# Modulation steps issued one by one behind weight tiles, and z gates multiplied in full float32

## The chip, the cores and the metric

The kernel runs on one core of a Trainium2 chip, as one program. The metric is the time of one execution in microseconds (us); a median of three runs is given with the lowest and the highest. All of the engines' times come from a profile of one execution.

## The reference, cut to what matters

Two blocks work on 256 tokens of width 1024. The first block has two layers. Each layer is a norm, one wide projection, three mixers beside each other, and an output projection. The mixers are an attention with compressed, selected and windowed keys (nsa), a linear recurrence (lru) and a convolution (conv). Each mixer's output is gated by its own `z` columns of the same wide projection:

```
h = rms_norm(x, norm_g[l]);  cols = h @ w_in[l]          # z_nsa, z_lru, z_conv among the columns
mixed = concat([y_nsa * silu(z_nsa), y_lru * silu(z_lru), y_conv * silu(z_conv)])   # 512 columns each
x = x + mixed @ w_out[l]
```

The second block starts from a modulation. It depends only on the conditioning vectors, not on x, and so can be computed at any time before the second block needs it:

```
mod_lat = silu(c) @ w_ada + b_ada         # 6 parts of 1024: sh1, sc1, gt1, sh2, sc2, gt2
mod_ctx = silu(c_ctx) @ w_ada + b_ada     # the same weights
h_lat = rmsnorm(x, g_norm1) * (1 + sc1) + sh1;   h_ctx = rmsnorm(ctx, g_norm1) * (1 + csc1) + csh1
x = x + gt1 * mixers(h_lat, h_ctx);   h2 = rmsnorm(x, g_norm2) * (1 + sc2) + sh2
x = x + gt2 * peer(h2)                    # 16 of 16384 expert rows per head and token, gathered
```

## The kernel before, in words

Activations lie transposed: 8 blocks of 128 channels (k) by 256 tokens. A weight tile is 128 x 1024 float32, 512 KB: for 128 output columns, all 8 k. SP issues every load of it (`wload`, L310 to L316), into five raw buffers (`w`); modulation tiles have two buffers of their own (`wm`).

Products of layers are made in three passes of a faster precision, fp32r. The norm's output is split into a high part `hh` and a low part `hl` (`norm_apply`, L449), and each weight tile likewise (`wsplit`, L318): ScalarE casts it to `wh` (L323), VectorE subtracts that from the raw tile into `wl` (L268). `mm3` (L350) then makes hh·wh, hh·wl and hl·wh for each k, 24 products per tile. A split leaves the raw buffer free as soon as both engines have read it; there are three buffers for each half.

A layer has 40 such tiles: glu, kv, q and u (20, for the mixers), z (12, in six `zpair`s, L755) and the output projection `woa` (8), whose remaining part `wob` (for the convolution) comes as four tiles of another shape. Between them stand the attention's small float32 products, the convolution's taps on VectorE (L262), its norm, and the scan of the recurrence.

The modulation's five parts that TensorE computes (`part`, L958) have 8 steps each: one 512 KB tile of `w_ada` per step and four products of 32 columns, one in each column group of the array, with `silc` (the activated conditioning vectors) as stationary operand; then a copy, two transposes and an addition that put the part into `modt`. (The sixth part is summed on VectorE from tiles in the raw buffers.)

The order on every engine is set by a scheduler that runs through the program's instructions by priority, a time that the code writes down (`at`, L246), and moves them by its own timeline of engines and loads. Before the change the parts had times of their own, `P["mt"]`, taken by a hook of the layers (L1665): the first three parts at 62, 80 and 170, the last two at 243 and 270. A loaded tile's priority lies 25 us (`ll`) ahead of its use, a split's 6 us (`sl`). `slot` hands out named places in memory in turn: `g6` holds the norm's whole output until it is split, and later the split input of `wob` (`mch`, `mcl`).

Of the kernel before, what the change touches and what calls it, by code (L numbers as in the profile page):

```python
# [9 lines left out]
F32R = mybir.dt.float32r  # L10
# [9 lines left out]
T = 256  # L20
# [209 lines left out]

P = dict(np=5, glu=14, kv=35, kk=40, q=41, cmp=46, cmpd=5, w1n=62, cv0=32, cvd=35, att=57, attd=5, mix=137, woa=131, ln=145, pw2=160, wob=138, mod=5, ll=25000, sl=6000, nm=3, mt=(62, 80, 170, 243, 270), sp=29, L0=10, L1=196, S=369, B=500, cx=125, h1=2, h2=6, X=16, lri=37, lnk=7, tp=2, tq=0, ta=0, ml=40, mld=2.6, rt=36, g0=-32, ga=104, gb=161, gc=157)

# [6 lines left out]
def program(tc, A, dbg=lambda *a: None, stop=99):  # L241
# [11 lines left out]
        return p.tile(list(shape), dt, name=f"{tag}_{cnt[0]}", tag=tag, **kw)  # L253

    def mm(out, lhsT, rhs, start, stop):
        pe.matmul(out, lhsT, rhs, start=start, stop=stop)  # L256

    def tr(out, in_, ident):
        pe.transpose(out, in_, ident)  # L259
# [90 lines left out]
    def mm3(out, pairs, first=True, last=True, late=False):  # L350

        n = len(pairs)
        for i, (ah, al, bh, bl) in enumerate(pairs):
            mm(out, ah, bh, first and i == 0, False)
            if late:
                mm(out, al, bh, False, False)
            else:
                mm(out, ah, bl, False, False)
                mm(out, al, bh, False, last and i == n - 1)
        if late:  # L360
            for i, (ah, al, bh, bl) in enumerate(pairs):
                mm(out, ah, bl, False, last and i == n - 1)

    def rsqrt(p, v, shape, tag, bufs=2):

# [80 lines left out]
    hh = mk(cp, [128, 8, T], F32R, tag="hh")  # L446
    hl = mk(cp, [128, 8, T], F32R, tag="hl")

    def norm_apply(p, src, gain, shift=None, hi=None, lo=None, bc=None):  # L449
        if bc is None:  # L450
            bc = norm_rstd(p, [src[:, k] for k in range(8)], D)
        g6 = None if hi is not None else slot("g6", 2048).rearrange("p (k t) -> p k t", k=8)
        if hi is None:
            hi, lo = hh, hl
        p0 = tc.cur_priority
        for k in range(0, 8, 2):
            tc.cur_priority = p0
            t = mk(p, [128, 2, T], tag="tmp2", bufs=2) if g6 is None else g6[:, k:k + 2]
            for q in range(2):
                scaled[:] = [dve.scalar_tensor_tensor(t[:, q], src[:, k + q], gain[:, k + q:k + q + 1], bc, op0=mul, op1=mul)]  # L460
            if shift is None:
# [12 lines left out]
        return last  # L474
# [88 lines left out]
    def layer(l, L, hook=lambda n: None):  # L563
# [8 lines left out]
        def proj2(i, t=None):  # L572

            acc = psum("acc", [128, 2, T])
            for q in range(2):
                if t is not None:
                    at(L + t + 2.6 * q)
                wh, wl = wsplit(A["w1"][l, i + q], [128, 8, 128])
                mm3(acc[:, q], [(wh[:, k], wl[:, k], hh[:, k], hl[:, k]) for k in range(8)], late=i == 0)
            if t is not None:  # L580
                at(L + t + 5.2)
            return acc
# [170 lines left out]
        gzc = slot("gz4", 1024).rearrange("p (i t) -> p i t", i=4)  # L753

        def zpair(i):  # L755
            acc = proj2(20 + i)
            th = mk(b1, [128, 2, T], tag="tmp2", bufs=2)
            act.activation(th, acc, AF.Tanh, scale=0.5)
            stt(gz[:, i:i + 2] if i < 8 else gzc[:, i - 8:i - 6], th, 1.0, acc, add, mul)
# [81 lines left out]
            onat.append(oT)  # L841


        g6 = slot("g6", 2048, F32R).rearrange("p (w i t) -> p w i t", w=2, i=4)
        mch, mcl = g6[:, 0], g6[:, 1]

        def pick(i):
            return (hh, hl, i) if i < 8 else (mch, mcl, i - 8)

        def msplit(i, src):  # L850
            h, lo, j = pick(i)
# [68 lines left out]
        for n in range(0, 8, 2):  # L920
            acc = psum("acc", [128, 2, T])
            for q in range(2):
                at(L + P["woa"] + 2.6 * (n + q))
                wh, wl = wsplit(A["woa"][l, n + q], [128, 8, 128])
                mm3(acc[:, q], [(wh[:, k], wl[:, k], hh[:, k], hl[:, k]) for k in (4, 5, 6, 7, 0, 1, 2, 3)])
            stt(XT[:, n:n + 2], acc, 0.5, XT[:, n:n + 2], mul, add)
            for c in order.pop(0):
                steps[c]()

        for n2 in range(4):  # L930
            at(L + P["wob"] + 2.6 * n2)
            wh, wl = wsplit(A["wob"][l, n2], [128, 4, 256])
            acc = psum("acc", [128, 2, T])
            for q in range(2):
                s = slice(q * 128, q * 128 + 128)
                mm3(acc[:, q], [(wh[:, k, s], wl[:, k, s], mch[:, k], mcl[:, k]) for k in range(4)])
            stt(XT[:, n2 * 2:n2 * 2 + 2], acc, 0.5, XT[:, n2 * 2:n2 * 2 + 2], mul, add)
# [6 lines left out]
    def modulation():  # L944

        sc = slot("silc", 256).rearrange("p (k w) -> p k w", k=8)

        def prep():
            nc.sync.dma_start(pb2, A["pb2"])
            cT = P2("c").rearrange("p (k w) -> p k w", w=2)  # L950
            pool.memset(sc, 0.0)
            s2 = sc[:, :, 0:2]
            act.activation(s2, cT, AF.Tanh, scale=0.5)
            stt(s2, s2, 1.0, cT, add, mul)
            ts(s2, s2, 0.5, None, mul)
            act.activation(sc0, sc[:, :, 0], AF.Copy)

        def part(m):  # L958
            acc = psum("c", [128, 256])
            for k in range(8):  # L960
                w = wload(A["wada"][m, k], [128, 4, 256], "wm", NWM, b1)
                for j in range(4):
                    pe.matmul(acc[32 * j:32 * j + 32], sc[:, k], w[:, j], start=k == 0, stop=k == 7,  # L963
                              tile_position=(0, 32 * j))
            rows = slot("ang", 256)
            act.activation(rows, acc, AF.Copy)
            tp = psum("c", [128, 2, 128])
# [12 lines left out]

        return [prep] + [lambda m=m: part(m) for m in (1, 0, 2, 4, 3)[:int(P["np"])]]

    def modsum(acc, m, k):

# [5 lines left out]
            stt(acc, w, s, acc, mul, add)  # L990

    def modparts():
        for m in (4, 3)[int(P["np"]) - 3:]:
            acc = mk(b1, [128, 1024], tag="wm", bufs=NWM)
            for k in range(8):
                modsum(acc, m, k)
# [661 lines left out]
            pass  # L1658
        pp.release()

    steps = modulation()
    at(P["mod"])
    steps.pop(0)()

    def hook(n, l):  # L1665
        if n == 0:
            if l == 1:
                next(two)
            return
        for i in range(min(int(P["nm"]), len(steps)) if l == 0 else len(steps)):  # L1670
            at(P["mt"][int(P["np"]) - len(steps)])
            steps.pop(0)()

    layer(0, P["L0"], lambda n: hook(n, 0))
    two = second(P["L1"] + P["cx"], P["S"])
# [18 lines left out]
```

## Time and profile before

| | us |
|---|---|
| median of 3 runs | 1381.29 (1377.42 to 1384.13) |
| the profiled execution | 1384.02, its span 1382.2 |
| TensorE (PE) busy | 1193.9, 86% of the span, mean granted clock 0.946 |
| VectorE (DVE) busy | 991.6, 72% |
| ScalarE (ACT) busy | 530.5, 38% |
| moved by DMA | 387.5 MB, 280 GB/s in the mean; 268.45 MB of it gathered expert rows |

The execution falls into parts: layer 0 up to about 248 us, layer 1 up to about 469, the second block's mixers up to about 640, then the experts. A busy share over the whole span mixes these; the table of stretches below separates them. A product's duration in the timeline overlaps the next one's, so the cost of one is read from start to start. A float32 product of TensorE appears as two records, an fp32r product as one.

### The profile page before, as it was taken

The page shows a single profiled execution, that of the slowest core. Times are in us where ns is not written, and L with a number is a line of the kernel's source. Part 1 is how long each engine was busy: PE and PEld are TensorE (multiplying, and loading weights), DVE is VectorE, ACT ScalarE, POOL GpSimd, SP SyncE. Part 2 cuts the span into 40 slices and gives each one's busy share as a digit, 9 for nine tenths or more (in the row PEclk, how much of TensorE's full clock was granted, in tenths as well). Part 3 has the DMA queues.
Part 4 walks back from the last instruction along what each step waited for, and adds up shares of the span by engine and source line. Part 5 has one row for each costly group of instructions (what it writes and reads, how often), then busy time and mean ns, then how long its engine had stood idle before and what let it go on. Part 6 is the DMA issues. An engine that isn't in the chain of part 4 may idle for free.

```text
span 1382.2 us, 17743 instructions
## 1 busy us (share of the span) xinstructions
PE 1193.9 (86%) x5972; PEld 775.5 (56%) x5972; DVE 991.6 (72%) x2440; ACT 530.5 (38%) x1136; POOL 296.2 (21%) x279
## 2 busy tenths in 40 slices
PE   6999889899979999999898877778887878778776
PEld 5987659698947986658794323343333333323332
DVE  6898865599988676566678776777766767676554
ACT  5635643344755555554543212222212222212211
POOL 0000000000000000000024444434453444444441
PEclk9999999899999999999999999999899999999999
DMA  8587454547413442401479999999999999999996
GB/s 321 196 282 274 158 183 168 197 158 264 137 41 100 153 130 83 146 16 46 138 313 387 422 422 421 421 409 384 421 414 422 421 419 397 424 421 398 421 422 263
DMA packets 71340, 387.50 MB, mean 280 GB/s; under 512 B 8402, under 2 KB 9426, under 8 KB 38227
## 3 DMA queue, kind: packets, MB, share of 16 engines
q0 software_dynamic: 36864, 268.45, 47.1%
q1 hardware_dynamic: 34386, 117.93, 24.7%
q8 instruction: 48, 0.79, 0.2%
q14 instruction: 42, 0.34, 0.1%
HBM read 385.30 MB, written 1.05 MB: 280 GB/s over the span
## 4 chain that ended last, share of the span: by engine, by line
PE 48%; DMA 30%; DVE 8%; issue 7%; POOL 4%; ACT 2%; POOLq 0%; DVEq 0%; SPq 0%; ACTq 0%
DMA G<-uv,eix 27%; PE acc L256 22%; PE acx L256 11%; PE s L256 5%; POOL G L1583 4%; DVE G L1586 4%; DMA wm<-wada 2%; PE c L963 2%; PE t L256 2%; PE o L256 2%; PE s L412 1%; PE t L259 1%; PE c L256 1%; PE o L811 1%; PE o L645 1%
## 5 line engine op out<-in xcount | busy, mean ns | idle before, releaser
L1586 DVE SCALAR_TENSOR_TENSOR G<-G,hn 128x1024 f32<-128x1024 f32 x256 | 313.4, 1224 | 177.3 <-DMA G<-uv,eix 170.2
L1583 POOL DMA_INDIRECT G<-uv,eix x256 | 288.7, 1128 | 438.8 <-PE acx L256 140.6
L268 DVE TENSOR_TENSOR wl<-w,wh 128x1024 fp32r<-128x1024 f32 (+2 forms) x142 | 171.4, 1209 | 69.8 <-ACT wh L323 68.3
L323 ACT ACTIVATE wh<-w 128x1024 fp32r<-128x1024 f32 (+2 forms) x142 | 148.5, 1048 | 188.1 <-PE acc L256 115.7
L256 PE MATMUL t<-G,dg 128*128 128x512 f32 x256 | 146.5, 656 | 70.1 <-ACT dg L1599 70.1
L256 PE MATMUL c<-G,dg 128*128 128x512 f32 x256 | 148.1, 663 | 62.4 <-ACT dg L1599 62.4
L256 PE MATMUL acc<-hh,wh 128*128 128x256 f32 x608 | 178.5, 297 | 7.8 <-ACT hh L468 3.6
L256 PE MATMUL acc<-hh,wl 128*128 128x256 f32 x608 | 176.8, 293 | 2.7 <-DVE wl L268 2.0
L256 PE MATMUL acc<-hl,wh 128*128 128x256 f32 x608 | 166.5, 287 | 1.2 <-DVE hl L268 1.1
L1599 ACT ACTIVATE dg<-cst,w 128x128 f32<-128x128 f32 x256 | 89.4, 394 | 149.1 <-PE o L256 64.4
L256 PE MATMUL acx<-G,dg 128*128 128x512 f32 x256 | 143.1, 643 | 0.0
L256 PE MATMUL o<-G,dg 128*128 128x512 f32 x256 | 141.2, 635 | 0.0
L1590 ACT ACTIVATE s<-s 128x4 f32<-128x4 f32 (+1 forms) x66 | 13.5, 205 | 325.2 <-DVE G L1586 325.2
L256 PEld LDWEIGHTS t<-G,dg 128*128 128x128 f32 x256 | 50.2, 206 | 149.9 <-ACT dg L1599 96.0
L256 PEld LDWEIGHTS acc<-hh,wh 128*128 128x128 f32 x608 | 119.3, 197 | 16.2 <-issue 4.7
L256 PEld LDWEIGHTS c<-G,dg 128*128 128x128 f32 x256 | 50.5, 209 | 135.1 <-ACT dg L1599 83.3
L256 PEld LDWEIGHTS acc<-hh,wl 128*128 128x128 f32 x608 | 119.7, 197 | 7.1 <-DVE wl L268 2.9
L256 PEld LDWEIGHTS acc<-hl,wh 128*128 128x128 f32 x608 | 113.8, 193 | 5.8 <-issue 3.2
L262 DVE SCALAR_TENSOR_TENSOR g<-lu,pb,g 128x256 f32<-128x256 f32 x264 | 115.0, 476 | 0.2
L256 PEld LDWEIGHTS o<-G,dg 128*128 128x128 f32 x256 | 53.2, 208 | 69.9 <-issue 69.9
L256 PEld LDWEIGHTS acx<-G,dg 128*128 128x128 f32 x256 | 52.7, 206 | 69.0 <-issue 69.0
L1054 POOL MEMSET lu<- 128x16 f32 x1 | 0.4, 447 | 401.9 <-DVE g L262 401.9
(512 smaller groups left out, 1947.6 us busy)
## 6 DMA issues: line engine op xcount, KB each, us to landing
w<-w SPq DMA_DIRECT2D x64, 512.0 KB, 4.6
wm<-wada SPq DMA_DIRECT2D x40, 512.0 KB, 4.5
wa<-cw SPq DMA_DIRECT2D x16, 512.0 KB, 5.1
w<-woa SPq DMA_DIRECT2D x16, 512.0 KB, 3.5
w<-wpq SPq DMA_DIRECT2D x16, 512.0 KB, 3.5
w<-w2t SPq DMA_DIRECT2D x12, 512.0 KB, 3.5
w<-wob SPq DMA_DIRECT2D x8, 512.0 KB, 4.6
w<-w2v SPq DMA_DIRECT2D x8, 512.0 KB, 3.8
```

Source lines behind the costliest of these rows:

```text
L256: pe.matmul(out, lhsT, rhs, start=start, stop=stop)
L259: pe.transpose(out, in_, ident)
L262: (e or dve).scalar_tensor_tensor(out, a, s, b, op0=op0, op1=op1)
L268: return (e or dve).tensor_tensor(out, a, b, op=op)
L323: act.activation(hi, w, AF.Copy)
L412: pe.matmul(acc[j:j + 32], ones[:, 0:32], sq[:, q] if square else srcs[i + q], start=i + q < 4, stop=i + q >= n - 4, tile_position=(0, j))
L645: pe.matmul(hps[32 * j:32 * j + 32], blk[:, q4 * 4 + j], w[:, j], start=q4 == 0, stop=q4 == 3, tile_position=(0, 32 * j))
L811: pe.matmul(ops[gs, jj:jj + step], vsw[kb][:, bi - 1, gs], p4[:, :, g, kb], start=bi == 1 and kb == 0 and jj == 0, stop=False, tile_positi ...
L963: pe.matmul(acc[32 * j:32 * j + 32], sc[:, k], w[:, j], start=k == 0, stop=k == 7, tile_position=(0, 32 * j))
L1583: pool.indirect_dma_start(out=G, out_offset=None, in_=A["uv"], in_offset=bass.IndirectOffsetOnAxis(ap=eix[b][:, h, k:k + 1], axis=0))
L1586: dot = dve.scalar_tensor_tensor(G[:, 0:D], G[:, 0:D], 1.0, hn[b], op0=mul, op1=mul, accum_out=s[:, j:j + 1])
L1599: act.activation(dg, ident, AF.Copy, scale=w[:, j:j + 1])
```

## The change

The z gates' tiles are no longer split. `zpair` loads the raw tile and multiplies it by the norm's unsplit output (`whole[0]`, the `g6` place), in float32: 8 products per tile, no cast and no subtraction. `g6` is therefore needed longer, and `mch` and `mcl` are allotted at their first use, not earlier.

The modulation loses its times. It becomes a list of 45 steps (`modq`: 40 of products, 5 ends of parts); after two of every three tiles of `w1`, z and `woa`, `fill` takes one step off the list and issues it right behind that tile's last product. Each step issues the load of the tile two steps ahead; the first two loads stand at the start of layer 0. The computation is otherwise the same. The core of the diff (`P` loses np, nm and mt; `mm` and `mm3` return their last instruction):

```diff
+    modq, tiles_done = [], [0]
+    def fill(end):
+        tiles_done[0] += 1
+        if modq and tiles_done[0] % 3:
+            p = tc.cur_priority
+            with tc.issue_after(end.ins):
+                modq.pop(0)()
+            tc.cur_priority = p
...
+        whole[:] = [g6]                                   # in norm_apply
...
-                mm3(acc[:, q], [(wh[:, k], wl[:, k], hh[:, k], hl[:, k]) for k in range(8)], late=i == 0)
+                fill(mm3(acc[:, q], [(wh[:, k], wl[:, k], hh[:, k], hl[:, k]) for k in range(8)], late=i == 0))
...
         def zpair(i):
-            acc = proj2(20 + i)
+            acc = psum("acc", [128, 2, T])
+            for q in range(2):
+                w = wload(A["w1"][l, 20 + i + q], [128, 8, 128])
+                for k in range(8):
+                    end = mm(acc[:, q], w[:, k], whole[0][:, k], k == 0, k == 7)
+                fill(end)
...
+        order = [(m, k) for m in (1, 0, 2, 4, 3) for k in range(8)]
+        def load():
+            if order:
+                m, k = order.pop(0)
+                loaded.append(wload(A["wada"][m, k], [128, 4, 256], "wm", NWM, b1))
+        def products(m, k):
+            if k == 0:
+                accs[m] = psum("c", [128, 256])
+            w = loaded.pop(0)
+            for j in range(4):
+                pe.matmul(accs[m][32 * j:32 * j + 32], sc[:, k], w[:, j], start=k == 0, stop=k == 7,
+                          tile_position=(0, 32 * j))
+            load()
         def part(m):
-            acc = psum("c", [128, 256])
-            for k in range(8):
-                w = wload(A["wada"][m, k], [128, 4, 256], "wm", NWM, b1)
-                for j in range(4):
-                    pe.matmul(acc[32 * j:32 * j + 32], sc[:, k], w[:, j], start=k == 0, stop=k == 7,
-                              tile_position=(0, 32 * j))
+            acc = accs[m]
...
-    steps.pop(0)()
+    prep()
+    at(P["L0"] + P["glu"])
+    load()
+    load()
+    modq.extend(steps)
```

What this does to the order is seen at three places. In the rows, `c<-wm,silc` is a product of a modulation step, `acc` and `acx` are accumulations of weight tiles, `s`, `t` and `o` pieces of the attention and the norms. The first place is TensorE's queue in layer 0's tail before the change, behind the last z tile: the start of the third modulation part.

```order
L256 MATMUL s_1738<-g_10_86 128x512
L256 LDWEIGHTS identb_74
L256 MATMUL s_1738<-cmaskb_76,identb_74 128x2x128
L963 MATMUL c_1216<-wm_1217,silc_103 32x256 x2
L811 MATMUL o_1272<-pTs_1554,vsw_1075 64x256 x2
L963 MATMUL c_1216<-wm_1217,silc_103 32x256 x2
L963 MATMUL c_1216<-wm_1223,silc_103 32x256 x4
L256 MATMUL s_1763<-g_10_86 128x512
L256 LDWEIGHTS identb_74
L256 MATMUL s_1763<-cmaskb_76,identb_74 128x2x128
L963 MATMUL c_1216<-wm_1229,silc_103 32x256 x4
L963 MATMUL c_1216<-wm_1235,silc_103 32x256 x4
```

There the steps of a part stand close together, whole, between pieces of the attention. After the change the second step of the same part stands further ahead, in the tenth z tile of layer 0 (`g_37_163` is the unsplit norm output, `w_1641` the raw tile).

```order
L256 MATMUL acc_1624<-g_37_163,w_1641 128x256
L999 MATMUL c_1614<-wm_1522,silc_103 32x256
L256 MATMUL acc_1624<-g_37_163,w_1641 128x256
L999 MATMUL c_1614<-wm_1522,silc_103 32x256
L256 MATMUL acc_1624<-g_37_163,w_1641 128x256
L999 MATMUL c_1614<-wm_1522,silc_103 32x256
L256 MATMUL acc_1624<-g_37_163,w_1641 128x256
L999 MATMUL c_1614<-wm_1522,silc_103 32x256
L256 MATMUL acc_1624<-g_37_163,w_1641 128x256
L832 MATMUL o_1435<-pTs_1487,vsw_1169 64x128 x4
L259 MATMUL t_1543<-cst_62,pr_1499 128x128 x4
```

The step is cut into its four products, each between two of the tile's products. The second place is the boundary of the layers in TensorE's queue, before the change: the last products of layer 0, the norm's sums and its scaling (`t<-dg`), and the first tile of layer 1.

```order
L963 MATMUL c_3634<-wm_3647,silc_103 32x256 x4
L963 MATMUL c_3634<-wm_3653,silc_103 32x256 x4
L412 MATMUL s_2674<-tmp_435_2685,cst_62 32x256 x2
L412 MATMUL s_2674<-tmp_436_2690,cst_62 32x256 x2
L256 MATMUL s_2697<-cst_62,tmp_2695 128x1 x2
L963 MATMUL c_3634<-wm_3659,silc_103 32x256 x4
L963 MATMUL c_3634<-wm_3665,silc_103 32x256 x4
L256 MATMUL t_2716<-dg_2717,cst_62 128x128
L256 MATMUL t_2716<-dg_2720,cst_62 128x128
L963 MATMUL c_3634<-wm_3671,silc_103 32x256 x4
L256 MATMUL acc_2740<-hh_81,wh_2743 128x256
```

Four steps of a part stand within the norm's chain there, and another ahead of the next layer's first product. The same place after the change:

```order
L256 MATMUL acc_2412<-g_355_1994,wl_2410 128x256
L424 MATMUL s_2438<-tmp_413_2449,cst_62 32x256 x2
L424 MATMUL s_2438<-tmp_414_2454,cst_62 32x256 x2
L256 MATMUL s_2461<-cst_62,tmp_2459 128x1 x2
L256 MATMUL t_2480<-dg_2481,cst_62 128x128
L256 MATMUL t_2480<-dg_2484,cst_62 128x128
L256 MATMUL acc_2504<-hh_81,wh_2507 128x256
L256 MATMUL acc_2504<-hh_81,wl_2509 128x256
```

The norm's chain stands alone; the steps have moved behind tiles of layer 1.

## Rows read from the trace of the kernel before

**Rows 1.** The page, chain that ended last: shares by engine, by line.

```profile
PE 48%; DMA 30%; DVE 8%; issue 7%; POOL 4%; ACT 2%; POOLq 0%; DVEq 0%; SPq 0%; ACTq 0%
DMA G<-uv,eix 27%; PE acc L256 22%; PE acx L256 11%; PE s L256 5%; POOL G L1583 4%; DVE G L1586 4%; DMA wm<-wada 2%; PE c L963 2%; PE t L256 2%; PE o L256 2%; PE s L412 1%; PE t L259 1%; PE c L256 1%; PE o L811 1%; PE o L645 1%
```

**Rows 2.** Stretches of core 0: busy time of each engine in each.

```profile
core 0: us, PE busy (x) PEld busy (x) DVE busy (x) ACT busy (x) POOL busy (x), PEclk, DMA share, GB/s
19.20:158.80 139.60, 139.58 (x1117) 120.14 (x1118) 123.55 (x271) 76.68 (x144) 0.00 (x0) 1.00 0.68 237
158.80:204.40 45.60, 38.11 (x309) 19.87 (x307) 34.34 (x113) 22.38 (x59) 0.00 (x0) 0.90 0.59 206
...
248.20:262.40 14.20, 9.61 (x70) 4.23 (x69) 9.05 (x27) 4.52 (x8) 0.00 (x0) 0.67 0.68 234
262.40:384.30 121.90, 121.90 (x978) 112.65 (x974) 110.07 (x226) 66.34 (x128) 0.00 (x0) 1.00 0.52 175
384.30:407.50 23.20, 15.29 (x76) 8.86 (x76) 21.36 (x63) 12.61 (x28) 0.45 (x1) 0.85 0.12 39
407.50:433.80 26.30, 23.12 (x172) 14.60 (x171) 18.43 (x67) 16.52 (x47) 0.00 (x0) 1.00 0.15 50
```

**Rows 3.** The chain, 158 to 206, then 206 to 265: start, us, what.

```profile
by line: DMA wm<-wada 37.6%; PE c L963 17.7%; PE s L256 14.6%; PE t L259 6.2%; PE o L811 6.1%; PE o L256 4.0%; PE acc L256 4.0%; PE s L412 2.3%; ACT pr L794 2.1%; PE acx L256 2.0%; PE c L259 1.8%; ACT ang L966 0.8%; issue 0.8%
...
by line: PE acc L256 52.9%; PE acx L256 22.2%; DMA wm<-wada 15.2%; PE c L963 8.0%; PE s L412 1.8%; issue 0.2%
...
217.39 11.51 PE acc L256 x96
...
255.07 3.88 DMA wm<-wada
```

**Rows 4.** DMA issues: line, KB each, median us to landing.

```profile
wm<-wada SPq DMA_DIRECT2D x40, 512.0 KB, 4.5
```

**Rows 5.** The chain behind layer 1's z tiles: ends of VectorE's run.

```profile
388.22 1.29 DVE g L268 x2
...
402.83 0.20 DVE pc L268
```

**Rows 6.** TensorE's timeline: start, us, line, operation, shapes, count.

```profile
543.59 1.99 PE L256 MATMUL acx<-tmp2b,w 128*128 128x256 f32 x8
545.51 1.04 PE L1245 MATMUL t<-g,cst 128*32 128x512 f32 x2
```

**Rows 7.** Lines of the splits: ns minimum, median, maximum of one.

```profile
L323 ACT ACTIVATE wh<-w x142: 672/1059/1084, 9.8 to 917.1; 128x1024 fp32r<-128x1024 f32 x136, 128x840 fp32r<-128x840 f32 x4, 128x560 fp32r<-128x560 f32 x2
...
L268 DVE TENSOR_TENSOR wl<-w,wh x142: 724/1224/1239, 18.0 to 918.2; 128x1024 fp32r<-128x1024 f32 x136, 128x840 fp32r<-128x840 f32 x4, 128x560 fp32r<-128x560 f32 x2
```

**Rows 8.** TensorE's timeline at modulation steps, layer 0 and boundary.

```profile
112.35 0.64 PE L963 MATMUL c<-wm,silc 128*32 128x256 f32 x8
112.92 0.38 PE L256 MATMUL acc<-hh,wh 128*128 128x256 f32 x1
113.14 0.28 PE L256 MATMUL acc<-hl,wh 128*128 128x256 f32 x1
...
115.04 0.62 PE L963 MATMUL c<-wm,silc 128*32 128x256 f32 x2
115.59 1.13 PE L256 MATMUL s<-g,g 128*128 128x256 f32 x4
...
258.99 1.08 PE L963 MATMUL c<-wm,silc 128*32 128x256 f32 x8 [1.36 <-DMA wm<-wada]
```

**Rows 9.** TensorE's timeline: both layers' tails, from the convolution's first sum.

```profile
180.86 0.62 PE L412 MATMUL s<-g,cst 128*32 128x256 f32 x2
...
204.38 0.78 PE L256 MATMUL acc<-hh,wh 128*128 128x256 f32 x1
...
411.86 0.64 PE L412 MATMUL s<-g,cst 128*32 128x256 f32 x8
...
428.33 1.05 PE L256 MATMUL o<-rows,kv 128*128 128x128 f32 x8
```

More of the change, by code (lines that the diff above doesn't have):

```diff
@@ L229, in pack @@
     return {k: np.ascontiguousarray(v) for k, v in o.items()}
-P = dict(np=5, glu=14, kv=35, kk=40, q=41, cmp=46, cmpd=5, w1n=62, cv0=32, cvd=35, att=57, attd=5, mix=137, woa=131, ln=145, pw2=160, wob=138, mod=5, ll=25000, sl=6000, nm=3, mt=(62, 80, 170, 243, 270), sp=29, L0=10, L1=196, S=369, B=500, cx=125, h1=2, h2=6, X=16, lri=37, lnk=7, tp=2, tq=0, ta=0, ml=40, mld=2.6, rt=36, g0=-32, ga=104, gb=161, gc=157)
+P = dict(glu=14, kv=35, kk=40, q=41, cmp=46, cmpd=5, w1n=62, cv0=32, cvd=35, att=57, attd=5, mix=137, woa=131, ln=145, pw2=160, wob=138, mod=5, ll=25000, sl=6000, sp=29, L0=10, L1=196, S=369, B=500, cx=125, h1=2, h2=6, X=16, lri=37, lnk=7, tp=2, tq=0, ta=0, ml=40, mld=2.6, rt=36, g0=-32, ga=104, gb=161, gc=157)
 ORDER = [",0,C1c,E2,,3s,B,,DF,Aw,x,,y,zp,q,,,", "C,0,c1,2F3w,,D,E,sB,,,,Ax,y,z,p,q,,"]
@@ L255, in mm @@
     def mm(out, lhsT, rhs, start, stop):
-        pe.matmul(out, lhsT, rhs, start=start, stop=stop)
+        return pe.matmul(out, lhsT, rhs, start=start, stop=stop)
     def tr(out, in_, ident):
@@ L358, in mm3 @@
                 mm(out, ah, bl, False, False)
-                mm(out, al, bh, False, last and i == n - 1)
+                end = mm(out, al, bh, False, last and i == n - 1)
         if late:
             for i, (ah, al, bh, bl) in enumerate(pairs):
-                mm(out, ah, bl, False, last and i == n - 1)
+                end = mm(out, ah, bl, False, last and i == n - 1)
+        return end
+    modq, tiles_done = [], [0]
[6 more added lines that the diff above has]
+            tc.cur_priority = p
     def rsqrt(p, v, shape, tag, bufs=2):
@@ L447, in program @@
     hl = mk(cp, [128, 8, T], F32R, tag="hl")
+    whole = []
     def norm_apply(p, src, gain, shift=None, hi=None, lo=None, bc=None):
@@ L841, in attend @@
             onat.append(oT)
-        g6 = slot("g6", 2048, F32R).rearrange("p (w i t) -> p w i t", w=2, i=4)
-        mch, mcl = g6[:, 0], g6[:, 1]
+        mc = []
         def pick(i):
-            return (hh, hl, i) if i < 8 else (mch, mcl, i - 8)
+            if i < 8:
+                return hh, hl, i
+            if not mc:
+                g6 = slot("g6", 2048, F32R).rearrange("p (w i t) -> p w i t", w=2, i=4)
+                mc.extend((g6[:, 0], g6[:, 1]))
+            return mc[0], mc[1], i - 8
         def msplit(i, src):
@@ L924, in layer @@
                 wh, wl = wsplit(A["woa"][l, n + q], [128, 8, 128])
-                mm3(acc[:, q], [(wh[:, k], wl[:, k], hh[:, k], hl[:, k]) for k in (4, 5, 6, 7, 0, 1, 2, 3)])
+                fill(mm3(acc[:, q], [(wh[:, k], wl[:, k], hh[:, k], hl[:, k]) for k in (4, 5, 6, 7, 0, 1, 2, 3)]))
             stt(XT[:, n:n + 2], acc, 0.5, XT[:, n:n + 2], mul, add)
@@ L932, in layer @@
             wh, wl = wsplit(A["wob"][l, n2], [128, 4, 256])
+            mch, mcl = mc
             acc = psum("acc", [128, 2, T])
@@ L956, in prep @@
             act.activation(sc0, sc[:, :, 0], AF.Copy)
-        def part(m):
-            acc = psum("c", [128, 256])
-            for k in range(8):
-                w = wload(A["wada"][m, k], [128, 4, 256], "wm", NWM, b1)
-                for j in range(4):
-                    pe.matmul(acc[32 * j:32 * j + 32], sc[:, k], w[:, j], start=k == 0, stop=k == 7,
-                              tile_position=(0, 32 * j))
+        loaded = []
+        order = [(m, k) for m in (1, 0, 2, 4, 3) for k in range(8)]
[3 more added lines that the diff above has]
+                loaded.append(wload(A["wada"][m, k], [128, 4, 256], "wm", NWM, b1))
+        accs = {}
+        def products(m, k):
[6 more added lines that the diff above has]
+            load()
+        def part(m):
+            acc = accs[m]
             rows = slot("ang", 256)
@@ L979, in part @@
                 stt(mg["pr"], modt[:, 32:40, 0], 1.0, P2("g2"), add, mul)
-        return [prep] + [lambda m=m: part(m) for m in (1, 0, 2, 4, 3)[:int(P["np"])]]
+        steps = []
+        for m in (1, 0, 2, 4, 3):
+            steps += [lambda m=m, k=k: products(m, k) for k in range(8)] + [lambda m=m: part(m)]
+        return prep, load, steps
     def modsum(acc, m, k):
@@ L992, in modparts @@
     def modparts():
-        for m in (4, 3)[int(P["np"]) - 3:]:
+        for m in ():
             acc = mk(b1, [128, 1024], tag="wm", bufs=NWM)
@@ L1659, in peer @@
         pp.release()
-    steps = modulation()
+    prep, load, steps = modulation()
     at(P["mod"])
-    steps.pop(0)()
-    def hook(n, l):
[L1666 to L1672, printed above, removed]
+    prep()
[3 more added lines that the diff above has]
+    modq.extend(steps)
+    def hook(n, l):
+        if n == 0 and l == 1:
+            next(two)
     layer(0, P["L0"], lambda n: hook(n, 0))
```

## The prediction

> **What bounds the kernel now.** I read the chain that ended last first. TensorE stands on 48% of it, gathers of expert rows on 27%, loads of the modulation's weights on 2%, VectorE on 8% [rows 1]. The table of stretches then says which engine holds which stage [rows 2]. The reader is to see full stretches and stretches with holes. In 19.20 to 158.80 TensorE is busy 139.58 of 139.60 us at clock 1.00, and in 262.40 to 384.30 all of 121.90: there a microsecond of TensorE work more is a microsecond more, and VectorE (123.55 and 110.07 us busy) is nearly as full behind it. In the tail of layer 0 (158.80 to 204.40), at the boundary of the layers (248.20 to 262.40) and behind layer 1's z tiles (384.30 to 433.80, in two rows) TensorE has holes, and the granted clock is down to 0.90, 0.67 and, until 407.50, 0.85. The end belongs to the experts' gathers, which no edit touches, so what happens earlier only shifts that stage.
>
> What TensorE waits for differs. In layer 0's tail the chain gives 37.6% of 48 us, 18.0 us, to loads of modulation weights, at the boundary 15.2% of 59 us, 9.0 us [rows 3]: the parts stand there as blocks, and a step eats a 512 KB tile in 0.6 us that takes 4.5 us to land [rows 4, 8]. Behind layer 1's z tiles it is VectorE, 14.8 us in one run from 388.22 to 403.03 (taps of the convolution, LRU scan, softmax pieces) [rows 5]. In the chain such a step is longer than TensorE's own idling, because products of other work run while the transfer is under way: the wait of 3.88 us that began at 255.07 left 1.36 us idle [rows 3, 8].
>
> **The sum.** What TensorE can win at all is its idle time and its slow clock. Idle, from rows 2: 45.60−38.11 = 7.5, 14.20−9.61 = 4.6, 23.20−15.29 = 7.9, 26.30−23.12 = 3.2, together 23.2 us. Clock: 38.11×0.10 = 3.8, 9.61×0.33 = 3.2, 15.29×0.15 = 2.3, together 9.3. So 32.5 us is the ceiling; against it stands the added work.
>
> Term A, the z tiles. An fp32r product of 256 columns takes 0.12 us (96 in 11.51 [rows 3]), a tile with its three products over 8 k 24×0.12 = 2.88. A full float32 product of the same shape is two records, 8 of them going by in 543.59 to 545.51, 0.24 each [rows 6]; a tile has 16, 3.84 us. So +0.96, times 24 tiles +23.0 us. In exchange each tile takes 1059 ns from ScalarE and 1224 ns from VectorE [rows 7], 25 and 29 us. In the full stretches these were beside TensorE, so there they buy nothing; they count where VectorE stands on the chain, in layer 1's run of 14.8 us.
>
> Term B, the modulation steps. They are the same 40 steps, but the order cuts them otherwise: counted in it, their products stand in 45 unbroken groups before and in 63 after, since several steps are now issued one product at a time between products of z tiles. A whole step (8 records) delays the next instruction by 112.92−112.35 = 0.57 us; a lone product (2 records) by 115.59−115.04 = 0.55 [rows 8]. The four column groups of a step run side by side, and a lone one pays for all. Hence 18×0.55 = +9.9 us. From below a lone product would be a quarter of a step, 0.14, and cutting would cost nothing: 0. From above it is 0.65 with a change of precision on top, +11.7. I take 9.9, the row that is exactly this case.
>
> The row says that a lone group costs as much as four. The Trainium skill, "TensorEngine Tiling (Array Packing)", Key Properties, says that going from one tiling mode to another (not from tile to tile) drains the engine, and that tiles work independently; both speak against this change, which alternates 32-column groups with full-width rows up to eight times in a step. By its words the cut is paid each time, as in the row, with a sum of +6.4 below; by counting products alone the sum would be −3.5.
>
> Term C, the changes between fp32r and float32. The next product after the float32 step at 112.35 starts at 112.92 and its successor only 0.22 later, against 0.12 within a tile [rows 3, 8]: 0.1 per change. The attention's products are float32, and so are the z tiles now; by the order 30 to 60 changes go, −3 to −6, taken as −4.5.
>
> TensorE work: 23.0+9.9−4.5 = +28.4 us.
>
> Term D, the waits that go, out of the 32.5. Layer 0's tail: from the convolution's first sum (180.86) to the first tile of the output projection (204.38) it takes 23.5 us; the same sequence in layer 1, which has no modulation in it, runs from 411.86 to 429.4, 17.5 us, of which about 3 are the context norm of the next block [rows 9]. So about 15 remain: −8.5 of the 11.3 there. Boundary: all eight steps of part 4 leave it, but the norm's chain of sums, square root and scaling stays, and nothing stands beside it any more that could hold TensorE at a high clock: −2 of 7.8. Behind layer 1's z tiles: twelve subtractions and twelve casts fewer ahead of the run (14.7 us of VectorE, 12.7 of ScalarE) and 11.5 us more of z products beside it. In the new order the taps end ahead of the z tiles, so the run should be covered: −11.5 of 13.4. Together −22; 10.5 us stay, mostly what late attention pieces wait for in each other. What is late next is the chain score, exponent, transpose, product at the end of each layer. The added load calls of the first steps lie on SP's queue behind one weight tile at the start and may cost 0 to 0.5 us; taken as 0. A step waits only for its own tile; behind it on TensorE's queue stands the next weight tile, and behind that the accumulation that VectorE reads.
>
> 28.4−22 = +6.4 us on the profiled execution of 1384.0 (span 1382.2 and 1.8 around it). That run lies 2.7 above the median of 1381.3, so the difference goes on the median: 1387.7, given as 1387.
>
> **Rivals.**
> First, everything goes: VectorE's 29 us are what really held the tail, lone products hide in the z products, and the whole 32.5 goes: 23.0−4.5−32.5 = −14, 1367; with the products at 0.55, 1377. For it speaks VectorE at 89 and 90% in the full stretches; against it, that TensorE was full there all the same.
>
> Second, lone products cost their quarter while D holds: 1378, no change. Against it speaks the row at 115.04.
>
> Third, slower: a z tile now keeps its raw buffer until its sixteenth product instead of until two splits have read it (2.3 us), and SP issues loads in order; a modulation tile queued behind a weight load without a free buffer comes late, and the step then stalls every tile behind it. Two of three tiles carry a step, one in 1.5×3.84 = 5.8 us, two tiles ahead, 11.5 us of lead; 4.5 us of landing leave 7. From 7 us of SP's waiting on, half of the 27 us of load waits would be back, +13.5: 1401. For it speaks that every z tile among 24 holds its buffer longer and that the steps now run where the weight loads are densest; against it, that the DMA shares of 0.68 and 0.52 in the full stretches leave the queues time. Its own range is 1394 to 1405.
>
> **How the numbers follow.** What a measurement of this kernel can tell from no change is about 0.5%, 6.9 us: 1374.4 to 1388.2. Forecast 0.45, with its own range 1381 to 1393 (B −9.9 to +1.8, D ±3.5, C ±1.5, not all at once); 55 of 100 of it lie within. First rival 0.18 (of which 0.16 below 1374.4), second 0.12 (0.10 within), third 0.25 (all above). Faster 0.16+0.02 = 0.18, same 0.25+0.10+0.02 = 0.37, slower 0.20+0.25 = 0.45. Range 1369 to 1400: it leaves out the far half of the third, 0.13, and what of the first lies under 1369, 0.06.
>
> **What the changed profile would show.** A: z products as 128x256 float32 at 0.24 us, 384 of them, and 24 fewer casts and subtractions. B: lone modulation products between z products with starts 0.5 us or more apart; about 0.14 would refute it. D: no waits of the chain for modulation tiles in layer 0's tail or at the boundary, about 15 us from the convolution's sum to the output projection, and no VectorE run of over 5 us behind layer 1's z tiles. The third rival would show as TensorE waiting for modulation tiles between z tiles. The prediction is wrong if TensorE's gain in idle time and clock up to 640 exceeds 35 us, or falls short of 15.

## The result, and the profile after

The changed kernel takes 1397.12 us (median of 4 runs, 1395.96 to 1400.39), the kernel before in the same comparison 1379.36 (1376.65 to 1384.13): ratio 1.0129, 95% interval 1.0093 to 1.0165. It is slower by 18 us, between 13 and 23. The forecast was 1387 in a range of 1369 to 1400, with slower as the likeliest of the three signs (0.45); the time lies within the third rival's own range (1394 to 1405), but, as shown below, not for its reason.

The page of the changed kernel's profiled execution (1396.8 us, span 1395.0): busy time of the engines, then the chain by engine and by line.

```profile
PE 1218.9 (87%) x5780; PEld 778.1 (56%) x5780; DVE 969.3 (69%) x2416; ACT 507.9 (36%) x1112; POOL 290.6 (21%) x279
...
PE 50%; DMA 28%; DVE 8%; issue 7%; POOL 4%; ACT 2%; POOLq 0%; DVEq 0%; SPq 0%; ACTq 0%
DMA G<-uv,eix 27%; PE acc L256 23%; PE acx L256 11%; PE s L256 5%; POOL G L1626 4%; DVE G L1629 4%; PE c L999 2%; PE o L256 2%; PE t L256 2%; PE t L259 1%; PE s L424 1%; PE c L256 1%; PE o L832 1%; DVE oh L268 1%; PE o L660 1%
```

TensorE is busy for 25 us more than before, VectorE for 22 and ScalarE for 23 less; the chain has TensorE on 50% (48% before), and loads of modulation weights are gone from its list [rows 1]. Where the time went is fixed by two rows of the gathers' line, first of before, then of the changed kernel; the last two numbers are the starts of the first and the last gather.

```profile
L1583 POOL DMA_INDIRECT G<-uv,eix x256: 932/938/1986, 700.0 to 1359.0; - x128
```

```profile
L1626 POOL DMA_INDIRECT G<-uv,eix x256: 932/937/1983, 712.1 to 1373.7; - x128
```

The first gather starts 12.1 us later, and from there to the last it takes 659 us before and 662 after. So the loss arises before the experts. (The remainder to 18 us is that the profiled execution of before was the slowest of its runs, and a scatter of 3 us in the gathers.) These are the stretches of the changed kernel, cut where the convolution's first sums begin in each layer, at the first tile of the output projection, and at layer 1's first tile; then the kernel before, cut in the same way (in layer 0 at the last group of these sums).

```profile
core 0: us, PE busy (x) PEld busy (x) DVE busy (x) ACT busy (x) POOL busy (x), PEclk, DMA share, GB/s
19.20:187.50 168.30, 168.09 (x1118) 127.45 (x1118) 132.15 (x316) 78.47 (x161) 0.00 (x0) 1.00 0.61 212
187.50:206.60 19.10, 15.19 (x110) 10.33 (x109) 14.21 (x56) 9.89 (x29) 0.00 (x0) 0.80 0.10 31
206.60:262.70 56.10, 50.61 (x378) 44.11 (x376) 28.85 (x46) 19.10 (x28) 0.00 (x0) 0.96 0.52 179
262.70:426.00 163.30, 163.27 (x1114) 129.69 (x1114) 128.31 (x298) 72.11 (x157) 0.13 (x1) 0.99 0.52 181
426.00:447.80 21.80, 18.90 (x142) 12.41 (x141) 14.38 (x52) 13.50 (x37) 0.00 (x0) 1.00 0.18 62
```

```profile
19.20:181.80 162.60, 158.06 (x1241) 127.91 (x1241) 144.01 (x327) 88.37 (x172) 0.00 (x0) 0.98 0.67 235
181.80:204.40 22.60, 19.62 (x186) 12.10 (x185) 13.87 (x57) 10.70 (x31) 0.00 (x0) 0.95 0.54 186
204.40:260.00 55.60, 51.01 (x400) 44.24 (x398) 29.45 (x47) 19.43 (x28) 0.00 (x0) 0.93 0.58 200
260.00:411.90 151.90, 143.99 (x1097) 125.22 (x1096) 137.27 (x305) 83.22 (x167) 0.45 (x1) 0.97 0.44 147
411.90:433.70 21.80, 18.62 (x141) 12.15 (x140) 14.89 (x54) 13.51 (x37) 0.00 (x0) 1.00 0.18 61
```

These answer to [rows 2], with cuts that fit the new order. Layer 0's body is 5.7 us longer, its tail 3.5 shorter, the stretch with the boundary 0.5 longer, layer 1's body 11.4 longer: 14.1 us up to the end of layer 1, of which the second block's mixers then take 2 back. Before, TensorE idled 4.5 and 7.9 us in the two bodies; now it is busy there all the time and at clock 1.00 or 0.99: the waits are gone, and more work has taken their place. What work, the timeline of TensorE in a z tile shows (start, us, then line, operation, shapes, count; a product of a modulation step, `c<-wm,silc`, is two records, and so is a z product).

```profile
118.14 0.68 PE L256 MATMUL acc<-g,w 128*128 128x256 f32 x2
118.75 0.62 PE L999 MATMUL c<-wm,silc 128*32 128x256 f32 x2
119.30 0.70 PE L256 MATMUL acc<-g,w 128*128 128x256 f32 x2
119.92 0.62 PE L999 MATMUL c<-wm,silc 128*32 128x256 f32 x2
120.47 0.70 PE L256 MATMUL acc<-g,w 128*128 128x256 f32 x2
```

From start to start, the lone product of a step takes 0.55 us, as in [rows 8]. But the z product between two of them takes 0.62, and in an undisturbed run of z products it is far less, as the next rows show: 26 records in 5.70 us, 0.219 each, 0.44 a product.

```profile
363.36 5.86 PE L256 MATMUL acx<-g,w 128*128 128x256 f32 x26
369.06 1.03 PE L256 MATMUL s<-g,g 128*128 128x256 f32 x4
```

So a lone product costs its own 0.55 and another 0.2 on the z products beside it. Counted in the two timelines, modulation products stand in 63 unbroken groups after the change, 29 of them lone ones; start to start they fill 34.3 us, against 27.6 before (idle time left out), part of which ran at the low clock of the holes.

### The profile page after: what moved, and what is told of

The parts are those of the page before. It is cut to its first block, busy times and chain, and to the rows that moved or that the text cites. A ratio compares the mean times of both kernels' runs of the same rounds, so it can differ in the third digit from the quotient of the medians.

```text
span 1395.0 us, 17263 instructions
## 1 busy us (share of the span) xinstructions
PE 1218.9 (87%) x5780; PEld 778.1 (56%) x5780; DVE 969.3 (69%) x2416; ACT 507.9 (36%) x1112; POOL 290.6 (21%) x279
## 4 chain that ended last, share of the span: by engine, by line
PE 50%; DMA 28%; DVE 8%; issue 7%; POOL 4%; ACT 2%; POOLq 0%; DVEq 0%; SPq 0%; ACTq 0%
DMA G<-uv,eix 27%; PE acc L256 23%; PE acx L256 11%; PE s L256 5%; POOL G L1626 4%; DVE G L1629 4%; PE c L999 2%; PE o L256 2%; PE t L256 2%; PE t L259 1%; PE s L424 1%; PE c L256 1%; PE o L832 1%; DVE oh L268 1%; PE o L660 1%
## 5 line engine op out<-in xcount | busy, mean ns | idle before, releaser
L1626 POOL DMA_INDIRECT G<-uv,eix x256 | 283.4, 1107 | 396.1 <-PE acx L256 124.1
L268 DVE TENSOR_TENSOR wl<-w,wh 128x1024 fp32r<-128x1024 f32 (+2 forms) x118 | 142.0, 1206 | 64.5 <-ACT wh L323 63.7
L323 ACT ACTIVATE wh<-w 128x1024 fp32r<-128x1024 f32 (+2 forms) x118 | 123.2, 1045 | 168.5 <-PE acc L256 103.4
L256 PE MATMUL acc<-hh,wh 128*128 128x256 f32 x480 | 145.2, 306 | 9.0 <-ACT hh L483 3.6
L256 PE MATMUL acc<-hh,wl 128*128 128x256 f32 x480 | 140.6, 296 | 1.3 <-DVE wl L268 1.3
L1633 ACT ACTIVATE s<-s 128x4 f32<-128x4 f32 (+1 forms) x66 | 13.5, 205 | 329.2 <-DVE G L1629 329.1
L256 PE MATMUL acc<-hl,wh 128*128 128x256 f32 x480 | 129.9, 287 | 0.0
L256 PEld LDWEIGHTS acc<-hh,wh 128*128 128x128 f32 x480 | 96.1, 201 | 18.7 <-issue 6.5
L256 PEld LDWEIGHTS acc<-hh,wl 128*128 128x128 f32 x480 | 96.2, 201 | 4.4 <-issue 2.0
L256 PEld LDWEIGHTS acc<-hl,wh 128*128 128x128 f32 x480 | 90.4, 196 | 1.8 <-issue 1.6
```

What stands on the lines that cost most here:

```text
L256: return pe.matmul(out, lhsT, rhs, start=start, stop=stop)
L268: return (e or dve).tensor_tensor(out, a, b, op=op)
L323: act.activation(hi, w, AF.Copy)
L1626: pool.indirect_dma_start(out=G, out_offset=None, in_=A["uv"], in_offset=bass.IndirectOffsetOnAxis(ap=eix[b][:, h, k:k + 1], axis=0))
```

## The experiments

All experiments were timed in 5 rounds against the kernel before. This table has what the readings rest on: the ratio, the start of the first gather from each profile (us), and layer 1's body from its first tile to the convolution's first sum, with the modulation steps in it.

| kernel | ratio (95%) | first gather | layer 1's body, steps in it |
|---|---|---|---|
| before | 1 | 700.0 | 151.9, 1 |
| changed | 1.0129 (1.0093 to 1.0165) | 712.1 | 163.3, 16 cut |
| float32 z tiles alone | 0.9933 (0.9906 to 0.9959) | 692.0 | 152.4, 8 |
| new places of the steps alone | 1.0109 (1.0076 to 1.0143) | 721.5 | 163.0, 16 cut |
| changed, whole steps | 1.0004 (0.9987 to 1.0020) | 700.6 | 157.7, 16 |
| changed, whole, none behind z | 0.9993 (0.9975 to 1.0010) | 701.5 | 158.1, 15 |
| new places, whole, split z | 1.0058 (1.0034 to 1.0083) | 709.7 | 159.0, 16 |
| float32 z, old places, whole and early | 1.0084 (1.0056 to 1.0111) | 709.4 | 145.8, 0 |
| whole, six at the boundary | 0.9983 (0.9961 to 1.0004) | 698.8 | 152.8, 11 |
| the same, last part held back | 0.9989 (0.9969 to 1.0009) | 697.8 | 152.9, 9 |
| whole, nine in the tail, six at the boundary | 0.9973 (0.9950 to 0.9996) | 692.8 | 154.2, 11 |
| float32 z, 5 of 40 steps | 0.9830 (0.9795 to 0.9865) | 678.0 | 145.9, 0 |
| split z, 5 of 40 steps | 0.9913 (0.9887 to 0.9940) | 685.6 | 151.4, 0 |

**One half of the change at a time.** The first run puts the z tiles alone into the kernel before (its `part` and hook unchanged):

```diff
-            acc = proj2(20 + i)
+            acc = psum("acc", [128, 2, T])
+            for q in range(2):
+                w = wload(A["w1"][l, 20 + i + q], [128, 8, 128])
+                for k in range(8):
+                    mm(acc[:, q], w[:, k], whole[0][:, k], k == 0, k == 7)
```

> The z gates' tiles in full float32, the modulation steps in the places they had before the change. Theory 1 (added TensorE work decides): the 24 z tiles cost about 21 us more than with splits, as the changed kernel's trace has it up to the second block, and give back only the run of VectorE behind layer 1's z tiles (some 8 to 10 us); the waits for modulation weights stay. So 8 to 14 us above the kernel before, about 1390. Theory 2 (the steps' new places are what costs, late loads and stalls behind them): the z tiles alone are near nothing, 1375 to 1383.

It is faster than the kernel before, by 0.67%, and so than both kernels compared so far: theory 1 was wrong on the z tiles, and by this run alone theory 2 looked right. Its stretches, with the same cuts as above:

```profile
19.20:172.80 153.60, 153.60 (x1082) 124.93 (x1081) 130.64 (x315) 75.46 (x157) 0.00 (x0) 0.99 0.63 221
172.80:195.30 22.50, 19.27 (x192) 11.20 (x192) 13.61 (x55) 11.12 (x31) 0.00 (x0) 1.00 0.66 216
195.30:249.80 54.50, 50.06 (x394) 44.03 (x392) 28.70 (x45) 19.46 (x28) 0.00 (x0) 0.95 0.60 207
249.80:402.20 152.40, 152.38 (x1049) 128.01 (x1049) 125.89 (x297) 71.78 (x156) 0.13 (x1) 0.99 0.49 168
```

Layer 0's body is 9.0 us shorter than before, layer 1's as long with eight steps in it where before had one; both are full. Part of the 9.0 is that seven steps have moved from layer 0's body to layer 1's (17 stand in layer 0's, 24 did before). The second run makes the other half, the steps in their new places with split z tiles (`acc = proj2(20 + i)` again in the changed kernel).

> The modulation steps in their new places, the z gates' tiles split as before. Theory 1: without the float32 tiles some 21 us of TensorE work go and VectorE's run in layer 1 returns; the cut steps still cost some 7 us and the waits for their weights are gone. About the kernel before, 1374 to 1383. Theory 2: nearly all of the loss stays, 1392 to 1398.

It keeps nearly all of the loss. What costs is in the steps, as theory 2 has it; but there are no late loads in its chain, so the mechanism was still open.

**Cut or whole.** In the changed kernel the four products of a step are given a higher priority, so that the scheduler sets them side by side:

```diff
+            p = tc.cur_priority
+            tc.cur_priority = 0
             for j in range(4):
                 pe.matmul(accs[m][32 * j:32 * j + 32], sc[:, k], w[:, j], ...
+            tc.cur_priority = p
```

> The changed kernel with a higher priority for the four products of a step, so that each of the 40 steps stands in one piece (40 groups of products, not 63). Theory 1: 23 groups fewer at 0.55 us, and as many float32 products fewer that pay 0.2 us for a change of the array's mode: 13 to 18 us below the changed kernel, about 1382. Theory 2: a step waits for its tile in one piece as in four, no change, 1394 to 1400. If a lone product costs only its quarter of a step: 1390 to 1394.

The ratio falls from 1.0129 to 1.0004, 1.25% or 17 us (12 to 23 by the two intervals), at the upper end of what theory 1 gave, and the intervals lie apart. The same tile as above, now with a whole step in it:

```profile
117.45 0.68 PE L256 MATMUL acc<-g,w 128*128 128x256 f32 x2
118.06 0.64 PE L1001 MATMUL c<-wm,silc 128*32 128x256 f32 x8
118.62 0.70 PE L256 MATMUL acc<-g,w 128*128 128x256 f32 x2
```

0.56 us for all four products. The z product ahead of the step still takes 0.61, so a group pays the 0.2 on its neighbours whether it is whole or lone; fewer groups pay it less often. Start to start, modulation products in the two layers' bodies fall from 31.5 to 20.1 us and z products from 89.9 to 86.0, and the groups in the timeline from 63 to 41: 15.4 us for 22 groups, 0.70 each, near the 0.55 and 0.2 of the rows. Late loads are not the cause: SP issues the same loads, in an order that differs at 6 of 238 places.

Up to the end of layer 1's body this trace is 19.4 us shorter than the changed kernel's (426.0 and 406.6), but its first gather is only 11.5 us earlier. Between them lie the second block's mixers, first of the changed kernel, then of this one:

```profile
426.00:712.10 286.10, 270.02 (x1697) 216.12 (x1697) 192.21 (x509) 153.24 (x311) 3.98 (x9) 0.98 0.30 100
406.60:700.60 294.00, 278.81 (x1696) 220.88 (x1696) 192.24 (x509) 153.97 (x311) 3.98 (x9) 0.94 0.29 97
```

The work is the same, and TensorE idles 16.1 and 15.2 us; what differs is the granted clock, 0.98 and 0.94. So the column of first gathers holds up to 8 us that a profiled execution's clock decides, and the kernels are better compared by ratio and by stretches. The next run takes the steps from behind the z tiles and lets one follow each of the remaining tiles (`fill` not called in `zpair`, `% 3` left out).

> The changed kernel with no step behind a z tile; one behind every other tile of the layers instead (two of three before). The steps then stand among fp32r tiles and nearly all in one piece (41 groups). Theory 1: as with whole steps, 1380 to 1386, for the float32 z tiles still cost their 21 us. Theory 2: tiles follow each other closer there, a step for each tile of 2.9 us against 4.3 us of landing with two buffers; if late loads are the cost, it grows: 1397 to 1410.

0.9993: as with whole steps. Half again as dense, behind split tiles alone, the loads still come in time, and behind which tile a whole step stands makes no difference that can be measured. With split z tiles, whole steps in the new places:

> Split z tiles, the steps behind the tiles as in the changed kernel, each step in one piece. If cutting the steps is the loss, some 14 to 17 us below the same kernel with cut steps (ratio to the kernel before 1.0109): ratio 0.997 to 1.001. If the placing of whole steps among full stretches still costs as it does with float32 z tiles (9 us above z tiles alone), and unsplit z tiles gain 8 us, ratio 1.005 to 1.009. If neither, 1.011.

1.0058, the second of the outcomes. So unsplit z tiles are worth 0.54% here too. With cut steps the two kernels can't be told apart (1.0129 and 1.0109), for there the cutting among their products ate the gain: cutting costs 0.5% with split z tiles and 1.25% with unsplit ones.

**What is left: places.** Whole steps in the new places are still 0.7%, some 9 us, above float32 z tiles alone. Whole steps in the old places (the same priority in `part`) should have told what the holes are worth:

> Float32 z tiles, the parts in their old places (no order tied to weight tiles), and a higher priority for a step's products: 40 whole steps, none at the boundary any more, 8 in layer 0's tail, the rest earlier. Against float32 z tiles alone (ratio 0.9933): nine groups of products fewer at 0.74 us, 6.7 us gained; the six steps of the boundary and eight of layer 1 now stand in layer 0. If steps in the holes were free, 14 steps x 0.6 less 6 already paid in layer 1, so some 4 us of loss against it: ratio 0.990 to 0.994. If holes are not free: 0.987 to 0.989.

Slower than all of these outcomes, and for another reason. With the highest priority the scheduler took every step as early as its loads allowed, all 40 in layer 0, and there TensorE did wait for them. Its timeline, two rows (in brackets: idle time before and what ended it):

```profile
162.58 1.08 PE L978 MATMUL c<-wm,silc 128*32 128x256 f32 x8 [4.92 <-DMA wm<-wada]
...
194.78 0.64 PE L978 MATMUL c<-wm,silc 128*32 128x256 f32 x8 [2.08 <-DMA wm<-wada]
```

This run shows the third rival's mechanism, in a kernel built otherwise; it says nothing of holes. It gives one thing: layer 1's body without any step, 145.8 us. The next run keeps the steps tied to tiles but for six at the boundary, which are issued behind layer 0's last `wob` product:

```diff
+        if l == 0:
+            hole(end, 6)          # six steps off modq, each issue_after(end.ins)
```

> As the changed kernel with whole steps, but six of the steps stand at the boundary of the layers, and the later steps move up by six. If the hole there (5.5 us idle, and a low clock) carries steps for nothing, six steps at 0.57 and a change of precision of 0.2 go from the full stretches: 4 to 5 us below whole steps behind tiles (ratio 1.0004): 0.9965 to 0.998. If the steps' loads come late there as they did before the change, TensorE waits 4 us for them: 1.000 and more.

0.9983, just past the edge of the first outcome, and not distinguishable from no gain against 1.0004. Its stretches show both halves of it, in the first row the one with the boundary, in the second layer 1's body; then the same of whole steps without this edit.

```profile
194.50:252.90 58.40, 53.59 (x419) 45.44 (x417) 29.71 (x49) 19.71 (x29) 0.00 (x0) 0.94 0.59 207
252.90:405.70 152.80, 152.80 (x1079) 127.32 (x1075) 126.17 (x295) 71.46 (x156) 0.13 (x1) 0.99 0.52 180
```

```profile
194.20:248.90 54.70, 49.19 (x378) 43.38 (x376) 28.89 (x47) 19.00 (x28) 0.00 (x0) 0.97 0.54 183
248.90:406.60 157.70, 157.70 (x1115) 129.05 (x1115) 128.17 (x298) 72.14 (x157) 0.13 (x1) 0.99 0.55 188
```

Layer 1's body is 4.9 us shorter, as expected, but 3.7 come back at the boundary, where the steps wait for their tiles, as before the change [rows 8]:

```profile
246.68 0.64 PE L1010 MATMUL c<-wm,silc 128*32 128x256 f32 x8 [1.89 <-DMA wm<-wada]
248.35 0.96 PE L1010 MATMUL c<-wm,silc 128*32 128x256 f32 x8 [1.02 <-DMA wm<-wada]
...
251.88 1.08 PE L1010 MATMUL c<-wm,silc 128*32 128x256 f32 x8 [1.42 <-DMA wm<-wada]
```

Then the last part held back (`len(modq) > 9` in `fill`, nine steps behind layer 1's last z pair):

> As the run before it in this list, and the last part is held back until layer 1's last z tile, so that it stands in layer 1's tail. If the tail's holes (3 us idle, chain of the attention) carry steps: eight steps at 0.6 to 0.77 less from the full stretch, 2 to 3 us back in the tail: another 2 to 4 us, ratio 0.994 to 0.996. If they lengthen the attention's chain: no change to the run before.

No change: in the trace only two of the eight steps landed in the tail, the others still stood in layer 1's body, so this run doesn't test the tail. The last of these keeps only the first two parts behind layer 0's tiles and places nine steps in its tail, six at the boundary, the rest behind layer 1's first tiles (in the trace seven of the nine start within the tail and four of the six ahead of layer 1):

> The changed kernel with whole steps: two parts behind layer 0's tiles as in it, nine steps in layer 0's tail, six at the boundary, the rest behind layer 1's first tiles. Against six steps at the boundary alone (ratio 0.9983) seven steps leave full stretches at 0.77 and cost 0.37 in the tail, 2.8 us: ratio 0.994 to 0.997. If loads in the tail come late as before the change: 0.998 to 1.001.

0.9973, just above the first outcome and below the second. Its first gather starts at 692.8, as early as with float32 z tiles alone, but over the timed runs it doesn't beat their 0.9933.

**Hardly any steps.** The two last runs leave out seven of eight steps of each part (`range(1)` for `range(8)` in `part`), with the rest in their old places, with unsplit and with split z tiles.

> Float32 z tiles, steps in their old places, but of each of the five parts only the first of eight steps is multiplied and loaded (35 of 40 steps left out; the modulation's values are then wrong). By the stretches of the traces the 40 steps cost some 24 us there (0.7 to 0.8 each in full stretches, 0.35 in the tail and at the boundary): 35 of them 21 us below float32 z tiles alone (ratio 0.9933): ratio 0.977 to 0.980. If steps in the holes are free and only the 25 in full stretches cost: 0.982 to 0.985. If the steps are hidden nearly everywhere: 0.988 and more.

> The kernel before with only the first of eight steps of each part (35 of 40 left out, as in the run above). Its distance to that run is what unsplit z tiles are worth with almost no steps in the way. If they pay by ending VectorE's run in layer 1 and the switches of precision, about 8 us as with all the steps: ratio 0.983 to 0.988. If they pay only because of the steps beside them, the two runs are equal, 0.977 to 0.980.

0.9830 is the second of its outcomes, steps nearly free in the holes; 0.9913 is none of the two given: few steps help split tiles less than was expected. Between them lie 0.83%. In the old places 35 steps so cost 1.0% with float32 z tiles and 0.9% with split ones. In the new places they cost 1.7% whole and 3.0% cut. And unsplit z tiles pay by themselves, with nearly no steps in the way. How, these rows show: the bodies with unsplit tiles, then with split ones, and what TensorE waits for in the latter.

```profile
19.20:166.40 147.20, 147.20 (x990) 124.47 (x990) 130.56 (x317) 76.26 (x160) 0.00 (x0) 0.98 0.54 185
166.40:184.40 18.00, 14.87 (x116) 9.64 (x115) 13.48 (x56) 10.69 (x30) 0.00 (x0) 0.85 0.00 1
184.40:238.80 54.40, 48.88 (x353) 45.21 (x351) 29.52 (x48) 19.07 (x27) 0.00 (x0) 0.91 0.43 146
238.80:384.70 145.90, 145.90 (x987) 126.13 (x988) 125.73 (x294) 71.27 (x155) 0.13 (x1) 0.98 0.45 153
```

```profile
19.20:175.30 156.10, 147.40 (x1102) 124.88 (x1101) 143.18 (x333) 88.99 (x177) 0.00 (x0) 0.96 0.51 174
...
246.10:397.50 151.40, 143.84 (x1083) 127.28 (x1085) 137.69 (x303) 83.34 (x168) 0.18 (x1) 0.95 0.44 147
```

```profile
375.55 0.45 PE L259 MATMUL t<-cst,pr 128*128 128x128 f32 x1 [4.42 <-DVE pr L265]
...
383.20 0.39 PE L256 MATMUL acc<-hl,wh 128*128 128x256 f32 x1 [1.58 <-DVE hl L268]
```

With split tiles TensorE idles 8.7 us in layer 0's body and 7.6 in layer 1's, there mostly behind VectorE (the two rows above are 6.0 of it); with unsplit ones it doesn't idle, does 2.1 us more in layer 1, and both bodies are shorter.

Layer 1's body prices a step. With float32 z tiles 145.9 without any; 152.4 with 8, some of them cut (6.5/8 = 0.81), 157.7 with 16 whole (11.8/16 = 0.74), 163.3 with 16 cut (17.4/16 = 1.09). In layer 0's tail nine steps of the first experiment cost 4.5 us against the row above (22.5 and 18.0) or 3.4 against the changed kernel (19.1), 0.4 to 0.5 each, and the stretch with the boundary is 54.5 with six steps and 54.4 without any.

## Why the prediction was right, and where not

The range and the sign with the largest chance held. The sum, +6.4, was 11 us short of the medians and 6 short of the two traces at the first gather, with errors of both signs.

Term A was too high, and so was A and C together (18.5). The row of eight float32 records held a change of mode, that is, of how the array's columns are grouped, to the 32-column rows beside it: in a longer run a record takes 0.219, not 0.24. A tile of 16 records then takes 3.50 us against 2.88, and A comes to 15. Measured in place it is less still: the 12 z tiles of layer 0 take 39 us before (106.7 for all split products, less 67.5 where only the z tiles are not split) and 43 unsplit, those of layer 1 37 and 42, together some 9. Why a split tile costs more than 2.88 there is only in part clear: narrow pieces between its products change the mode.

Term C has no cost behind it. Its 0.1 was read behind a step, where the mode changes too. Between full-width products of the kernel before, the change of precision is free: the float32 and the first fp32r products of these rows take 0.98 us from 349.39 to 350.37, and apart they would take 4×0.219+0.12 = 1.00.

```profile
349.39 1.02 PE L256 MATMUL s<-g,g 128*128 128x256 f32 x4
350.06 0.47 PE L256 MATMUL acx<-hl,wh 128*128 128x256 f32 x1
350.37 0.28 PE L256 MATMUL acx<-hh,wl 128*128 128x256 f32 x1
```

Term B failed in its size. Its price of a lone product, 0.55, was right, with the row to show it, but a group costs another 0.2 on its neighbours, so that 18 groups come to 13.5, not 9.9. (The 45 groups before count steps apart that stand back to back; the unbroken ones are 36 in the trace.) And 18 isn't the number that the cut deserves: against whole steps 22 groups fewer were worth 17 us. The Trainium skill, "TensorEngine Tiling (Array Packing)", Key Properties, has going between tiling modes drain the engine; the trace agrees in that each change costs, with 0.2 us on the full-width products and four groups in 0.56 where one takes 0.55.

Term D, −22, held as to the waits for modulation tiles, and VectorE's run in layer 1 is covered: next to no idle time in 262.70 to 426.00. It failed as to the holes: the tail gave back 3.5 us, not 8.5, and the boundary nothing. By the ten rows of the two kernels, idle time falls from 23.2 to 12.5 us and what the low clock costs by some 5, together 16 up to there where D has 22, just above the 15 below which the prediction called itself wrong. A step costs 0.4 to 0.5 in the tail, next to nothing at the boundary of the first experiment, and 0.74 behind a tile; I priced them at the same 0.57 in both, so that moving some fifteen of them into full stretches was free in my sum. The run with six put back at the boundary shows that this hole isn't always free either: 4.9 us won in the body, 3.7 paid at the boundary, where loads come late. With 15 for A, nothing for C, 13.5 for B and −16 for D the sum would have been +12.5, an estimate from these rows, beside 12.1 at the first gather and 14.1 at the end of layer 1: that the sum came as near as it did is in part luck, for A was 8 too high and the other three terms 4 to 6 too low each.

The third rival fell: the changed kernel's chain holds no wait for a modulation tile up to the second block, nor does the chain with a step behind each split tile. That its time was near is chance. One other load did come late, a compression weight in layer 0; here is its step in the chain, and the product that needs it in the timeline.

```profile
104.71 6.09 DMA wa<-cw
```

```profile
110.84 0.64 PE L660 MATMUL o<-wa,blk 128*32 128x256 f32 x8 [0.18 <-DMA wa<-cw]
```

TensorE had other products to do and idled 0.18 us. The first rival was half right: VectorE did hold the bodies, and unsplit z tiles pay, 0.5 to 0.8%, wherever steps aren't cut among their products. The second, lone products at a quarter of a step, is refuted by the row.

Not settled: why the gathers take between 654 and 662 us from the first to the last start, in kernels that don't differ there, and why the clock granted in the second block differs, with 286 to 294 us for its mixers; differences of a few microseconds between two kernels are not explained here.

## What to carry to other kernels

Work for a waiting engine is priced where it stands: a piece that is nearly free in a hole costs its full time, and a change of mode on either side, in a stretch that the same engine fills. When a scheduler may cut a small group of products that share the array, look in the order for lone ones among products of another shape, and tie the group together; here that was worth some 17 us by one priority. And a product that takes TensorE a fifth longer (3.5 against 2.88 us a tile) can win when the casts and subtractions that it saves belong to the engine that is waited for.

## What the runs showed of the hardware that was not expected

Four products of 32 columns in four column groups take 0.56 us side by side, one alone 0.55, and a full-width float32 product between two lone ones takes 0.62 instead of 0.44. Where whole steps stand between fp32r tiles, the products of these tiles cost more as well: in layer 1's body 73.4 us with 16 steps, 71.3 without any. Between full-width products, going from float32 to fp32r costs nothing that the starts show. And the same second block, with the same idle time, takes 286 us at a mean clock of 0.98 and 294 at 0.94.
